# Branch B of a hybrid decoder layer: who joins the transposed halves of P, and at which slots

## The chip, the cores and the metric

The kernel runs on one core of a Trainium2 chip. A core has five engines that run their own instruction queues in order and wait for each other through semaphores: TensorE (PE in the profile, with its weight loads as PEld), VectorE (DVE), ScalarE (ACT), GpSimd (POOL) and SyncE (SP), which here issues most of the transfers. The metric is the device time of one execution in microseconds (us), lower is better.

## The reference

One decoder layer over 512 tokens of width 2048, all in float32. One projection of the normalised input feeds three token mixers side by side, and their outputs are gated, projected, weighted and summed:

```python
proj = hn @ w_in                      # 512 x 2048 by 2048 x 12300
ya = sliding_window_attention(...)    # A: 12 query heads, 4 key heads, window 128
yb = forgetting_attention(...)        # B: 12 heads of 64, causal over all 512 tokens
yc = memory_attention(...)            # C: 4 heads of 128 over 256 memory tokens
y = g0 * (ya*silu(za) @ w_a) + g1 * (yb*silu(zb) @ w_b) + g2 * (yc*silu(zc) @ w_c)
return x + y @ w_out
```

The change touches branch B alone. For each of its 12 heads

```python
sc = q @ k.T * scale + c_q[:, None] - c_k[None, :]   # c: running sum of log forget gates
p = softmax(where(key <= query, sc, NEG))            # 512 x 512, causal
out = p @ v                                          # 512 x 64
```

## The kernel before, in words

**The stream and its clock.** TensorE works through one long stream of projection products (line 301): a unit is 24 matmuls, a value is split into a high and a low part, and a product takes three matmuls (high by high, high by low, low by high). A chunk of eight units makes one 512 x 384 or 512 x 512 block of the projection, in four PSUM banks that ScalarE (and for V also VectorE) evicts at its end. The next chunk writes the same banks. While the stream runs, attention work is slipped in by a clock that counts the stream's own matmuls: every three of them are a tick of half a slot, so a slot is six matmuls of the stream. What is due by the clock is written at that place into every engine's queue, so a slot number fixes the order of instructions in each queue, and no time. The order is manual: no scheduler changes it.

**The stages.** The 12 heads of B run in two halves of six. The first half runs while the chunks qB1, kB1 and vB1 are computed (24 units, 96 slots), the second half while qA0, qA1 and kvA are computed (again 96 slots). `BASES_B` gives each head its base slot within such a stage, `STEPS_B` the offset of each of its steps from that base.

**A head of B, step by step.** Offsets are those of the kernel before, in slots from the head's base.
- GpSimd builds the four blocks of bias `biB` (lines 621 and 622, offsets -2 to 1.5). They have two buffers, so the third waits until VectorE has used the first.
- At 0, 1, 3.5 and 5, for four blocks of 128 queries: TensorE makes the scores `sB` (lines 585 and 586), VectorE adds the bias and finds the row minimum into `pB` (line 609), ScalarE exponentiates (line 612, one slot later), VectorE divides by the row sum (lines 589 and 590, three slots later).
- `halves`: GpSimd copies the 32-bit values of `pB` as 16-bit numbers into `s1B` (lines 632 and 634), all the low halves of the words first and then all the high ones, so that each can be transposed as 16-bit data.
- `send`, 10.5: SyncE issues one transposing transfer (line 639) from `s1B` to `s2B`.
- `join`, 16.5: a copy (line 645) puts the two transposed halves together again, into 32-bit words in `ptB`: 128 x 2560 16-bit values, read in a row and written with every second place left out.
- `s2`, 18: ScalarE casts `ptB` to the high part `phB` (line 651). `s2l`, 19: VectorE subtracts it for the low part `plB` (line 654).
- `s3`, 20.5: TensorE makes eight products with V into `avB` (line 663), by turns with `phB` and `plB`. ScalarE copies the lower half of the bank out (line 575, `avsB`, one slot later) and VectorE adds the halves (line 579, 3.5 slots after that).

**What is shared.** `phB` and `plB` have one buffer, as have `s1B`, `s2B` and `ptB`. V (the tile `V`) has one buffer too, which the first half's heads read and which the eviction of vB1 at the stage's end writes anew. In the same queues stand, for each unit, ScalarE's cast of the next weights (line 212) and VectorE's low part of them (line 215), and for each query and key chunk the evictions (line 446), squares (line 411), sums (lines 415, 416), GpSimd's power (line 382) and VectorE's scaling (line 422).

Of the kernel before, what the change touches and what calls it, by code (L numbers as in the profile page):

```python
# [31 lines left out]
UK = 2  # L32
BOFF = (0, 512, 1024, 896)

BASES_B = ((14, 26, 38, 46, 58, 70), (14, 26, 38, 46, 58, 70))
BASES_A = (12.5, 17, 23.5, 37.5, 43, 48.5, 52, 70.5, 75.0, 79.5, 81, 89)
BASES_C = (12.0, 19.5, 28.0, 33.5)
STEPS_B = (-12, -8.5, -2, -1.5, 0, 1, 1.0, 1.5, 3.5, 5, 10.5, 16.5, 18, 19, 20.5, 4.5)
STEPS_A = (-5.0, -1.0, -0.5, -1.5, 6.5, 8, 11, -6.5)
STEPS_C = (-8, -3.5, 0.5, 1, 8.0, 4.5, 10)  # L40

# [16 lines left out]
def tile_hybrid_block(ctx, tc, xT, x, memT, mem, ng, mng, w_in, b_forget, gqa, gka, sinks, gqb, gkb, gqc, gkc,  # L58
                      w_mem, w_a, w_b, w_c, w_out, relm, out):
    nc = tc.nc  # L60
    ve, ac, po, pe, sy = nc.vector, nc.scalar, nc.gpsimd, nc.tensor, nc.sync
# [7 lines left out]
    def f32(ap):  # L69
        return ap.bitcast(F32)  # L70
# [15 lines left out]
    def ysv(br, i):  # L86

        if (br, i // 2) not in ys:
            ys[br, i // 2] = place({"B": 0, "A": 3, "C": 6}[br] + i // 2, f"ys{br}{i // 2}")
        return ys[br, i // 2][:, i % 2, :]  # L90
# [52 lines left out]
    def later(dt, f):  # L143
        at_slot(clock[0] + dt, f)
# [16 lines left out]
    def release(*names):  # L161
        for n in names:
            free[n] += 1
# [227 lines left out]
    def u16(ap):  # L391
        return ap.bitcast(U16)

    def spare(n, name, dtype=F32, cols=1280):

        return tokp.tile([P, 1280 * 4 // mybir.dt.size(dtype)], dtype, tag=f"X{n}", bufs=1, name=name)[:, :cols]
# [134 lines left out]
    def sbank(name):  # L531
        return bank(1, name)

    def avbank(name):
        return bank(0, name)
# [35 lines left out]
    def pv_out(av, dst, half, name, slots):  # L571

        def copy():
            tmp = tokp.tile([P, 512], F32, tag="sc", bufs=2, name=name)
            ac.copy(tmp[0:64, :], av[64:128, :])
            later(slots[1], lambda: add(tmp))

        def add(tmp):
            ve.tensor_tensor(dst, av[0:64, :], tmp[0:64, :], op=ALU.add)
            release("T")  # L580
        later(slots[0], copy)

    def scores(dst, q, kh, kl, i, ks):
        qs = slice(i * P, (i + 1) * P)
        pe.matmul(dst, q[:, qs], kh[:, ks], start=True, stop=False)
        pe.matmul(dst, q[:, qs], kl[:, ks], start=False, stop=True)

    def scaled(p, den, i, engine=po):
        ve.reciprocal(den[:, 4 + i:5 + i], den[:, i:i + 1])  # L589
        engine.tensor_scalar(p, p, den[:, 4 + i:5 + i], None, op0=ALU.mult)  # L590

    def head_B(h, kv):

        s = {}

        def s1(i):
            q, kh, kl, v, hv, cb = kv()
            if i == 0:
                s["p"] = at.p.tile([P, 1280], F32, tag="P", bufs=2, name=f"pB{h}")
                s["den"] = cp.tile([P, 16], F32, tag="den", bufs=2, name=f"denB{h}")  # L600
            p, den = s["p"], s["den"]
            o = (0, 128, 384, 768)[i]
            n = (i + 1) * P
            bi = s["b", i]
            sb = sbank(f"sB{h}_{i}")
            scores(sb[:, :n], q, kh, kl, i, slice(0, n))
            pi = p[:, o:o + n]
            nm = den[:, 8 + i:9 + i]
            ve.tensor_tensor_reduce(out=pi, in0=sb[:, :n], in1=bi[:, :n], scale=-1.0, scalar=3.0e38,  # L609
                                    op0=ALU.add, op1=ALU.min, accum_out=nm)  # L610
            release("bias")
            later(EXP_B, lambda: ac.activation(pi, pi, AF.Exp, bias=nm, scale=-1.0, accum_out=den[:, i:i + 1]))  # L612
            later(DIV_B, lambda: scaled(pi, den, i, ve))
            s["p", i] = pi
            if i > 1:
                later(DIV_B + 0.5, lambda: halves(i))

        def sb(i):
            n = (i + 1) * P
            bi = at.p.tile([P, S], F32, tag="bias", bufs=2, name=f"biB{h}_{i}")  # L620
            po.tensor_scalar(bi[:, :n], kv()[5][:, :n], -1.0, cq[:, i, h:h + 1], op0=ALU.mult, op1=ALU.add)
            po.affine_select(out=bi[:, i * P:n], in_=bi[:, i * P:n], pattern=[[-1, P]], compare_op=ALU.is_ge,
                             fill=NEG, base=0, channel_multiplier=1)
            s["b", i] = bi

        def halves(i):

            if i == 0:
                s["s1"] = spare(0, f"s1B{h}", U16, 2560).rearrange("p (e j n) -> p e j n", e=2, n=P)
            src = u16(s["p", i]).rearrange("p (j n e) -> p e j n", n=P, e=2)  # L630
            n = min(i + 1, 3)
            po.tensor_copy(s["s1"][:, :, i:i + 3 * n - 2:3, :], src[:, :, :n, :])
            if i == 3:
                po.tensor_copy(s["s1"][:, :, 7:8, :], src[:, :, 3:4, :])
                release("P")

        def send():
            s["s2"] = spare(1, f"s2B{h}", U16, 2560)
            sy.dma_start_transpose(out=s["s2"].rearrange("p (x n) -> p x n", n=P),
                                   in_=s["s1"].rearrange("p e j n -> p (e j n)"))  # L640
            release("S1")

        def join():
            s["t"] = spare(2, f"ptB{h}")
            ac.copy(u16(s["t"]).rearrange("p (n e) -> p e n", e=2), s["s2"].rearrange("p (e n) -> p e n", e=2))  # L645
            release("S2")

        def s2():
            s["hi"] = at.p.tile([P, 1280], F32R, tag="PH", bufs=1, name=f"phB{h}")
            s["lo"] = at.p.tile([P, 1280], F32R, tag="PL", bufs=1, name=f"plB{h}")  # L650
            ac.copy(s["hi"], s["t"])

        def s2l():
            ve.tensor_tensor(s["lo"], s["t"], f32(s["hi"]), op=ALU.subtract)
            release("RW")

        def s3():
            q, kh, kl, v, hv, cb = kv()
            av = avbank(f"avB{h}")
            for j in range(NT):  # L660
                n = S - j * P
                for w, t in enumerate((s["hi"], s["lo"])):
                    pe.matmul(av[:, j * P:], v[:, j, hv, :], t[:, BOFF[j]:BOFF[j] + n],  # L663
                              start=(j == 0 and w == 0), stop=(j == NT - 1 and w == 1))
            pv_out(av, ysv("B", h // 2)[(h % 2) * 64:(h % 2) * 64 + 64, :], h % 2, f"avsB{h}", PV_B)

        def done():
            release("Q", "KH", "KL", *(["cb"] if h % 2 else []))

        o = STEPS_B  # L670
        steps = [(o[2], ["bias"], lambda: sb(0)), (o[3], ["bias"], lambda: sb(1)), (o[4], ["P"], lambda: s1(0)),
                 (o[5], [], lambda: s1(1)), (o[6], ["bias"], lambda: sb(2)), (o[7], ["bias"], lambda: sb(3)),
                 (o[8], [], lambda: s1(2)), (o[15], ["S1"], lambda: (halves(0), later(0.5, lambda: halves(1)))), (o[9], [], lambda: (s1(3), done())),
                 (o[10], ["S2"], send), (o[11], ["RW"], join), (o[12], ["PT"], s2), (o[13], [], s2l),
                 (o[14], ["T"], lambda: (s3(), release("PT")))]
        return steps
# [119 lines left out]
    def plan(bases, heads):  # L796

        t0 = clock[0]
        for base, steps in zip(bases, heads, strict=True):
            Chain(t0 + base, steps)  # L800

    def heads_B(part):
        cache = {}

        def prep(pr, which):
            if which == "q":
                cb = at.p.tile([P, 2, S], F32, tag="cb", bufs=2, name=f"cb{part}{pr}")
                for e in range(2):
                    h = part * 6 + 2 * pr + e
                    sy.dma_start(out=cb[:, e, :], in_=cdram[h:h + 1, :].partition_broadcast(P))  # L810
                cache[pr, "c"] = cb
            src = toks[f"{which}B{part}"]
            tb = heads_T(src, pr * P, NT, f"t{which}B{part}{pr}")
            f, g = (q_stack, "qb") if which == "q" else (k_stack, "kb")
            cache[pr, which] = [f(tb, e, gains[g], f"{which}B{part}{pr}{e}") for e in range(2)]
            later(LOW_Q if which == "q" else LOW_K, lambda: release("T"))

        def mk(hl):
            def kv():
                q, k = cache[hl // 2, "q"][hl % 2], cache[hl // 2, "k"][hl % 2]  # L820
                return q, k[0], k[1], toks[f"vB{part}"], hl, cache[hl // 2, "c"][:, hl % 2, :]
            base = BASES_B[part][hl]
            pre = [(PREP_Q[part][hl // 2] - base, ["T", "Q", "Q", "cb"], lambda: prep(hl // 2, "q")),
# [752 lines left out]
    for e in range(2):  # L1576
        kt = at.p.tile([P, S], F32R, name=f"kl{e}", tag=f"kl{e}")
        po.memset(f32(kt[64:128, :]), 0.0)
        klt.append(kt)
    plan(BASES_B[0], heads_B(0))  # L1580
    run(n_p1, n_p2)
    plan(BASES_B[1], heads_B(1))
    run(n_p2, n_p3)
# [56 lines left out]
```

## Time and profile before

| | |
|---|---|
| time, median of 3 runs | 1539.13 us (1537.29 to 1539.95) |
| the profiled execution: its time | 1539.29 us |
| the profiled execution: its span | 1537.5 us |
| PE busy in the span | 1485.7 us (97%) |
| DVE, ACT, POOL busy | 1094.1, 761.6, 217.2 us |
| mean granted TensorE clock | 0.983 of full speed |

The span is the time from the first to the last instruction, so 1.8 us of the execution lie around it. The profile counts a matmul that is pipelined behind another as busy for its whole length, so a busy PE is not a PE at its peak. Times in the trace count from the start of the span. The two halves of branch B lie between 109.3 and 426.2 us: the chunk qB1 begins at 109.32, qA0 at 265.60, and the next chunk after kvA at 426.22.

### The profile page before, as it was taken

How to read it: one execution, taken by the hardware profiler on the slowest of the kernel's cores; microseconds unless marked ns; L12 is line 12 of the kernel's file. 1: busy time of each engine (PE TensorE's matmuls, PEld its weight loads, DVE VectorE, ACT ScalarE, POOL GpSimd, SP SyncE). 2: the span in 40 equal slices, each digit the busy share in tenths (PEclk: the TensorE clock that was granted, in tenths of full speed). 3: DMA queues.
4: the chain of work that ended last, by engine and by line, in shares of the span. 5: the costliest groups of instructions: out<-in, count | busy, mean ns of one | idle time of the engine just before them, and what ended most of it. 6: DMA issues, size and time to landing. Idle time of an engine off the chain costs nothing.

```text
span 1537.5 us, 20169 instructions
## 1 busy us (share of the span) xinstructions
PE 1485.7 (97%) x7073; PEld 1276.1 (83%) x7073; DVE 1094.1 (71%) x1862; ACT 761.6 (50%) x1200; POOL 217.2 (14%) x283
## 2 busy tenths in 40 slices
PE   9999778978999999999999999999999999999998
PEld 9998778977778888888888888888888888888887
DVE  5485555565567876657978787878787655679997
ACT  5546465556555766445544444444444444336442
POOL 0122441243223433000000000000000021110000
PEclk9999799988999999999999999999999999999999
DMA  8774334534434522358667676767676867775784
GB/s 281 222 223 113 100 86 131 151 86 114 137 107 139 163 83 86 93 192 262 224 188 251 195 250 194 252 191 251 193 247 191 292 180 236 250 239 192 253 284 154
DMA packets 166733, 287.35 MB, mean 187 GB/s; under 512 B 53596, under 2 KB 93148, under 8 KB 166632
## 3 DMA queue, kind: packets, MB, share of 16 engines
q1 hardware_dynamic: 161592, 269.54, 56.3%
q10 hardware_dynamic: 5040, 16.53, 3.2%
q8 instruction: 55, 0.90, 0.3%
q14 instruction: 46, 0.38, 0.1%
HBM read 244.58 MB, written 31.48 MB: 180 GB/s over the span
## 4 chain that ended last, share of the span: by engine, by line
PE 88%; ACT 6%; DVE 3%; issue 2%; POOL 1%; DMA 0%; SPq 0%; DVEq 0%; POOLq 0%; ACTq 0%
PE P L1113 40%; PE z L301 11%; PE uB L1113 4%; PE uA L1113 4%; PE qB L301 4%; PE vB L301 3%; PE kB L301 3%; PE qC L301 3%; PE uC L1113 3%; PE qA L301 3%; PE mem L301 3%; PE kvA L301 2%; ACT ptB L645 2%; PE avB L663 1%; DVE wc L215 1%
## 5 line engine op out<-in xcount | busy, mean ns | idle before, releaser
L215 DVE TENSOR_TENSOR wc<-wa,wb 128x512 fp32r<-128x512 f32 (+2 forms) x252 | 148.7, 629 | 110.4 <-ACT wb L212 105.3
L212 ACT CAST wb<-wa 128x512 fp32r<-128x512 f32 (+2 forms) x252 | 130.4, 566 | 132.2 <-PE z L301 34.5
L1155 ACT CAST wa<-rawl 128x1024 fp32r<-128x1024 f32 x85 | 89.5, 1053 | 207.5 <-DVE rawl L1045 158.4
L1045 DVE TENSOR_TENSOR rawl<-rawl 128x512 f32<-128x512 f32 x256 | 177.0, 692 | 5.7 <-DMA rawl<-in_w_out_dram 1.3
L1158 DVE TENSOR_TENSOR wc<-rawl,wa 128x1024 fp32r<-128x1024 f32 x85 | 105.0, 1235 | 52.0 <-ACT wa L1155 50.3
L1429 POOL TENSOR_TENSOR y<-y,gA 128x512 f32<-128x512 f32 x16 | 28.1, 1786 | 727.6 <-DVE gA L1427 727.6
L1158 DVE TENSOR_TENSOR we<-rawl,wd 128x512 fp32r<-128x512 f32 (+1 forms) x128 | 122.1, 954 | 4.1 <-ACT wd L1155 0.5
L1155 ACT CAST wd<-rawl 128x512 fp32r<-128x512 f32 (+1 forms) x128 | 106.8, 835 | 22.7 <-DVE rawl L1045 17.2
L301 PE MATMUL z<-ah,wb 128*128 128x512 f32 x256 | 101.9, 398 | 1.5 <-DVE V_vA L462 1.5
L301 PE MATMUL z<-ah,wc 128*128 128x512 f32 x256 | 99.9, 390 | 0.0
L301 PE MATMUL z<-al,wb 128*128 128x512 f32 x256 | 99.9, 390 | 0.0
L1155 ACT CAST wb<-rawl 128x1024 fp32r<-128x1024 f32 x43 | 45.3, 1054 | 87.8 <-DVE rawl L1045 70.5
L1113 PE MATMUL P<-wd,xhx 128*128 128x512 f32 x192 | 74.7, 389 | 0.0
L1113 PE MATMUL P<-wd,xlx 128*128 128x512 f32 x192 | 74.7, 389 | 0.0
L1113 PE MATMUL P<-we,xhx 128*128 128x512 f32 x192 | 74.7, 389 | 0.0
L1158 DVE TENSOR_TENSOR wb<-rawl,wb 128x1024 fp32r<-128x1024 f32 x43 | 52.5, 1222 | 25.6 <-ACT wb L1155 25.3
L1042 DVE TENSOR_TENSOR R<-P,R 128x512 f32<-128x512 f32 (+1 forms) x90 | 57.0, 673 | 6.9 <-PE P L1113 6.2
L301 PEld LDWEIGHTS z<-ah,wb 128*128 128x128 f32 x256 | 48.1, 188 | 11.2 <-DVE V_vA L462 1.9
L301 PEld LDWEIGHTS z<-ah,wc 128*128 128x128 f32 x256 | 48.1, 188 | 10.3
L590 POOL TENSOR_SCALAR pA<-pA,denA 128x256 f32<-128x256 f32 (+1 forms) x48 | 44.6, 946 | 78.8 <-DVE denA L589 78.8
L301 PEld LDWEIGHTS z<-al,wb 128*128 128x128 f32 x256 | 48.2, 188 | 9.0
L612 ACT ACTIVATE pB<-pB,denB 128x128 f32<-128x128 f32 (+3 forms) x48 | 27.0, 562 | 56.7 <-DVE denB L609 56.6
(411 smaller groups left out, 4287.9 us busy)
## 6 DMA issues: line engine op xcount, KB each, us to landing
rawl<-in_w_in_dram SPq DMA_DIRECT2D x144, 512.0 KB, 4.3
rawl<-in_w_out_dram SPq DMA_DIRECT2D x48, 512.0 KB, 4.9
wa<-in_w_in_dram SPq DMA_DIRECT2D x62, 384.0 KB, 3.6
wa<-in_w_in_dram SPq DMA_DIRECT2D x64, 256.0 KB, 3.0
rawl<-in_w_in_dram SPq DMA_DIRECT2D x48, 256.0 KB, 4.1
gates<-R ACTq DMA_DIRECT2D x24, 512.0 KB, 7.7
wa<-in_w_in_dram SPq DMA_DIRECT2D x16, 512.0 KB, 3.7
wa<-in_w_mem_dram SPq DMA_DIRECT2D x16, 512.0 KB, 3.6
```

The costliest lines, as they stand in the source:

```text
L212: ac.copy(hi[:, :n], raw[:, i, :n])
L215: ve.tensor_sub(lo[:, :n], raw[:, i, :n], f32(hi[:, :n]))
L301: pe.matmul(pb, a, m, start=b in fresh, stop=last and not todo[b])
L590: engine.tensor_scalar(p, p, den[:, 4 + i:5 + i], None, op0=ALU.mult)
L612: later(EXP_B, lambda: ac.activation(pi, pi, AF.Exp, bias=nm, scale=-1.0, accum_out=den[:, i:i + 1]))
L645: ac.copy(u16(s["t"]).rearrange("p (n e) -> p e n", e=2), s["s2"].rearrange("p (e n) -> p e n", e=2))
L1042: ve.tensor_tensor(out, a, b, op=ALU.add)
L1045: ve.tensor_tensor(out, a, b, op=ALU.subtract)
L1113: pe.matmul(*args, **kw)
L1155: ac.copy(hi[:, :k, :], src)
L1158: return lambda: ve.tensor_tensor(lo[:, :k, :], src, f32(hi[:, :k, :]), op=ALU.subtract)
L1429: po.tensor_tensor(y, y, g, op=ALU.add)
```

## The change

Two things are changed. `join` runs on GpSimd instead of ScalarE. And the slots: `join` is one slot earlier after its head's base (15.5 for 16.5), the cast `s2` one later (19 for 18), the subtraction `s2l` 1.5 later (20.5 for 19), and the products with V `s3` 4.5 later (25 for 20.5). The fifth head of each half begins one slot earlier (57 for 58) and the sixth two (68 for 70). Every step before `join` keeps its offset from its head's base.

```diff
-BASES_B = ((14, 26, 38, 46, 58, 70), (14, 26, 38, 46, 58, 70))
+BASES_B = ((14, 26, 38, 46, 57, 68), (14, 26, 38, 46, 57, 68))
-STEPS_B = (-12, -8.5, -2, -1.5, 0, 1, 1.0, 1.5, 3.5, 5, 10.5, 16.5, 18, 19, 20.5, 4.5)
+STEPS_B = (-12, -8.5, -2, -1.5, 0, 1, 1.0, 1.5, 3.5, 5, 10.5, 15.5, 19, 20.5, 25, 4.5)
@@ def join():
             s["t"] = spare(2, f"ptB{h}")
-            ac.copy(u16(s["t"]).rearrange("p (n e) -> p e n", e=2), s["s2"].rearrange("p (e n) -> p e n", e=2))
+            po.tensor_copy(u16(s["t"]).rearrange("p (n e) -> p e n", e=2), s["s2"].rearrange("p (e n) -> p e n", e=2))
             release("S2")
```

What this does to the queues is shown at three places. The numbers behind names are buffer numbers.

ScalarE in the first stage, where chunk qB1 ends and kB1 begins. `t_qB` are the evictions of its banks (`qB_2` and `qB_3` the third and fourth), the four rows of `kB` the keys of the third and fourth head, `pB` an exponential of the second head, `ptB` and `phB` the first head's join and cast. Before:

```order
L645 COPY ptB_1628<-s2B_1539 128x2x1280
L446 ACTIVATE t_qB_1603<-qB_2_1240,rstds 128x384
L558 ACTIVATE kB_1650<-tkB_1645,g_kb 64x512
L561 ACTIVATE kB_1650<-tkB_1645,g_kb 64x512
L558 ACTIVATE kB_1653<-tkB_1645,g_kb 64x512
L561 ACTIVATE kB_1653<-tkB_1645,g_kb 64x512
L446 ACTIVATE t_qB_1603<-qB_3_1241,rstds 128x384
L411 ACTIVATE sq_qB_1661<-t_qB_1603 128x384
L612 ACTIVATE pB_1557,denB_1558<-pB_1557,denB_1558 128x512
L651 CAST phB_1664<-ptB_1628 128x1280
L212 CAST wb_1667<-wa_1595 128x384 x2
```

The same place now:

```order
L446 ACTIVATE t_qB_1603<-qB_2_1240,rstds 128x384
L558 ACTIVATE kB_1650<-tkB_1645,g_kb 64x512
L561 ACTIVATE kB_1650<-tkB_1645,g_kb 64x512
L558 ACTIVATE kB_1653<-tkB_1645,g_kb 64x512
L561 ACTIVATE kB_1653<-tkB_1645,g_kb 64x512
L446 ACTIVATE t_qB_1603<-qB_3_1241,rstds 128x384
L411 ACTIVATE sq_qB_1661<-t_qB_1603 128x384
L612 ACTIVATE pB_1557,denB_1558<-pB_1557,denB_1558 128x512
L212 CAST wb_1664<-wa_1595 128x384 x2
L651 CAST phB_1690<-ptB_1613 128x1280
```

The join no longer stands ahead of the evictions, and the cast stands behind the next weights' cast.

GpSimd at the same time, now: `biB` are the last two biases of the second head, `ptB` the join of the first, `s1B` the second head's halves, `nr_qB` a power for the chunk's normalisation.

```order
L621 TENSOR_SCALAR biB_2_1574<-cb_1245,cq 128x384
L622 AFFINE_SELECT biB_2_1574<-biB_2_1574 128x128
L621 TENSOR_SCALAR biB_3_1582<-cb_1245,cq 128x512
L622 AFFINE_SELECT biB_3_1582<-biB_3_1582 128x128
L645 COPY ptB_1613<-s2B_1539 128x2x1280
L632 COPY s1B_1630<-pB_1557 128x2x128
L632 COPY s1B_1630<-pB_1557 128x2x2x128
L632 COPY s1B_1630<-pB_1557 128x2x3x128
L382 TENSOR_TENSOR nr_qB_1605<-nr_qB_1605,mhalf 128x6
```

Before, the row of `ptB` was not in this queue, and the rest stood in the same order. So the join now stands ahead of all the halves of the next head.

TensorE at the end of the first stage, now: the first bank of vB1 is complete, and the products with V of the sixth head come next, still with the old V.

```order
L301 MATMUL vB_0_2228<-wb_2556,ah_80 128x384
L301 MATMUL vB_0_2228<-wc_2557,ah_80 128x384
L301 MATMUL vB_0_2228<-wb_2556,al_88 128x384
L663 MATMUL avB_2606<-phB_2545,V_vB_1191 128x512
L663 MATMUL avB_2606<-plB_2546,V_vB_1191 128x512
L663 MATMUL avB_2606<-phB_2545,V_vB_1191 128x384
```

Before, the sixth head's products stood 2.5 slots (15 matmuls of the stream) earlier, ahead of the end of that bank. In both kernels every head's products stand exactly at base plus offset: none was pushed to a later slot by a tile or bank that was still taken.

## The prediction

> **What bounds the kernel now.** I read the page's slices first, to see where PE isn't full, then the stages, then who PE waits for.
>
> ```profile
> PE   9999778978999999999999999999999999999998
> PEclk9999799988999999999999999999999999999999
> ```
>
> One slice is 38.4 us. PE is full everywhere but in slices 5 to 10, and the granted clock drops in slices 5, 9 and 10: that is branch B. The stages (columns: length, then busy time and instructions of PE, PEld, DVE, ACT, POOL, then clock, DMA share, GB/s):
>
> ```profile
> 0.00:109.30 109.30, 107.14 (x597) 105.12 (x598) 65.82 (x158) 55.56 (x108) 16.68 (x25) 1.00 0.76 239
> 109.30:265.60 156.30, 132.73 (x699) 126.45 (x697) 84.20 (x205) 86.82 (x152) 52.63 (x86) 0.91 0.42 114
> 265.60:426.20 160.60, 140.82 (x697) 126.43 (x697) 94.69 (x222) 89.64 (x156) 50.45 (x83) 0.93 0.43 119
> 500.00:600.00 100.00, 99.49 (x536) 84.14 (x535) 72.06 (x201) 68.84 (x166) 42.13 (x46) 1.00 0.36 109
> ```
>
> The two B stages last 156.3 + 160.6 = 316.9 us and PE is busy for 273.6 of them, so 43.3 us are idle. No other engine is above 60% there, and transfers move half of what they do in the first stage. So PE is held up by order and latency. The last row, with branch A's heads, shows that PE can be full with DVE at 72%. Who PE waits for in 109.3 to 426.2 (total us, times, longest):
>
> ```profile
> PE avB L663 <- DVE plB L654: 24.5, 11, 2.7
> PE avB L663 <- ACT phB L651: 10.0, 8, 2.7
> PE qA L301 <- ACT t_qA L446: 3.1, 2, 2.5
> PE kB L301 <- ACT t_qB L446: 3.1, 2, 2.5
> PE vB L301 <- ACT t_kB L446: 1.5, 1, 1.5
> PE kvA L301 <- ACT t_qA L446: 0.8, 1, 0.8
> ```
>
> These six rows are 43.0 us, all of the idle time. 34.5 us are waits of the products with V for their two operands. The other 8.5 are waits for evictions at the ends of chunks.
>
> The idle time has a second price. PE from 178 to 188 us:
>
> ```profile
> 178.62 0.49 PE L663 MATMUL avB<-phB,V_vB 128*128 128x512 f32 x1 [2.67 <-ACT phB L651]
> 181.50 0.79 PE L663 MATMUL avB<-plB,V_vB 128*128 128x512 f32 x1 [2.38 <-DVE plB L654]
> 185.93 0.52 PE L301 MATMUL kB<-wb,ah 128*128 128x384 f32 x1
> 186.25 0.52 PE L301 MATMUL kB<-wc,ah 128*128 128x384 f32 x1
> 187.68 0.33 PE L301 MATMUL kB<-wb,ah 128*128 128x384 f32 x1
> 187.85 0.33 PE L301 MATMUL kB<-wc,ah 128*128 128x384 f32 x1
> ```
>
> After two waits matmuls start 0.32 us apart, and 0.17 apart from 187.5 on. The trace has nine such stretches, all between 153 and 382 us. Asked for as windows, the first and the sum:
>
> ```profile
> 153.30:163.50 10.20, 7.23 (x23) 6.38 (x22) 6.27 (x14) 4.33 (x9) 6.77 (x9) 0.50 0.45 104
> sum 51.20, PE 41.97 PEld 38.98 DVE 24.27 ACT 14.93 POOL 26.48; mean PE 4.66 PEld 4.33 DVE 2.70 ACT 1.66 POOL 2.94
> ```
>
> For 51.2 us the clock is at half, and PE works in 42.0 of them, so they cost 21.0 us.
>
> **The change part by part.** First, why the products wait. The three steps before them take, for one head:
>
> ```profile
> L645 ACT COPY ptB<-s2B 128x2560 uint16<-128x2560 uint16 x12 | 37.3, 3107 | 0.0
> L651 ACT CAST phB<-ptB 128x1280 fp32r<-128x1280 f32 x12 | 15.1, 1254 | 0.1
> L654 DVE TENSOR_TENSOR plB<-ptB,phB 128x1280 fp32r<-128x1280 f32 x12 | 17.8, 1485 | 0.0
> L215 DVE TENSOR_TENSOR wc<-wa,wb 128x384 fp32r<-128x384 f32 x79 | 41.7, 568 | 37.3 <-ACT wb L212 37.1
> ```
>
> The first three make 3.1 + 1.25 + 1.49 = 5.85 us in a row, without any queueing; a pair of weight subtractions (the fourth row, 1.1 us) can stand ahead of the low part. From join to products the old slots leave 20.5 - 16.5 = 4 slots. A slot is six stream matmuls of 0.17 us, so 1.03 us; with the heads' own matmuls it is on average (316.9 - 43.3 - 21.0)/192 = 1.32 us, from the two stages' 192 slots. 4 slots are 4.1 to 5.3 us: too few by 0.6 to 1.7 us even with empty queues, and the measured 34.5/12 = 2.9 us a head adds the queues.
>
> **Later products.** Now there are 25 - 15.5 = 9.5 slots, 9.8 us of the stream alone and 12.5 with the average of the heads' matmuls. They have to hold the join on GpSimd, 1.25, 1.1 and 1.49 us.
>
> **The join on GpSimd** is in no row. The nearest are GpSimd's own 16-bit copies, which read with a stride and write in a row, and what ScalarE pays for writing with a stride:
>
> ```profile
> 135.28 0.83 POOL L632 COPY s1B<-pB 128x768 uint16<-128x768 uint16 x1 [1.56 <-DVE pB L590]
> 136.05 0.40 POOL L634 COPY s1B<-pB 128x256 uint16<-128x256 uint16 x1
> L1503 ACT COPY y4s<-yh 128x512 uint16<-128x512 uint16 x8 | 6.2, 773 | 12.5 <-DMA yh<-gC 12.3
> L1155 ACT CAST wa<-rawl 128x1024 fp32r<-128x1024 f32 x85 | 89.5, 1053 | 207.5 <-DVE rawl L1045 158.4 <-PE P L1113 37.9 <-PE uA L1113 5.6
> L1429 POOL TENSOR_TENSOR y<-y,gA 128x512 f32<-128x512 f32 x16 | 28.1, 1786 | 727.6 <-DVE gA L1427 727.6
> ```
>
> From 256 to 768 values GpSimd takes 0.43/512 = 0.84 ns a value and 0.19 us at the start: 2560 values make 2.3 us, the lower bound. ScalarE's joins go from 773 ns for 512 to 3107 for 2560, 1.14 ns a value, its plain casts from 1053 ns for 1024 to 1254 for 1280, 0.79 ns: strided 16-bit writes cost it 1.45 times. With that factor GpSimd's join is 0.19 + 2560 x 0.84 x 1.45 = 3.3 us. The upper bound is GpSimd's dearest streaming row, the add of two operands, 1786/512 = 3.5 ns a value: 8.9 us. I take 3.3 us, since type and kind of copy are the same. Then 3.3 + 1.25 + 1.1 + 1.49 = 7.1 us of the 9.8: **all 34.5 us of waits go**, with 2.7 us to spare, and the cast isn't held up either (it stands 3.5 slots, 3.6 us, behind the join).
>
> **Is the join's data there a slot earlier?** The first head's last scores, and the transfer's median from issue to landing:
>
> ```profile
> 130.83 0.39 PE L585 MATMUL sB<-kB,qB 128*128 128x512 f32 x1
> s2B<-s1B SPq DMA_TRANSPOSE x12, 4.1
> ```
>
> That head's halves end at 136.05 + 0.40 = 136.45 us, so the data lands at 140.6, 9.8 us after the scores; the join stands 15.5 - 5 = 10.5 slots behind them, 10.8 us and more. It fits by 1 us or more.
>
> **What stands behind the join on GpSimd.** It is the next head's halves, then biases, then powers.
>
> ```profile
> POOL s1B L632 <- DVE pB L590: 82.5, 29, 9.5
> ```
>
> GpSimd waits 82.5 us for DVE before halves, so it has the room: 103.1 us busy of 316.9, plus 12 x 3.3 = 40 makes 143 of some 258. In the worst place (third head's join between the fourth head's halves) a 3.3 us join moves the fourth head's transfer by that much, and that head's join still stands 5 slots behind its transfer. Cost nothing. If that cover is gone, the late transfer holds the join, and a rival below prices it. DVE and ACT: DVE's 178.9 us stay, 69% of the shorter stage; ACT loses 37.3 of 176.5.
>
> **The evictions at chunk ends** waited behind the join on ACT:
>
> ```profile
> 145.31 3.10 ACT L645 COPY ptB<-s2B 128x2560 uint16<-128x2560 uint16 x1
> 148.29 0.56 ACT L446 ACTIVATE t_qB<-qB,rstds 128x384 f32<-128x384 f32 x1
> 148.76 0.67 ACT L558 ACTIVATE kB<-tkB,g_kb 64x512 fp32r<-64x512 f32 x1
> 151.53 0.58 ACT L446 ACTIVATE t_qB<-qB,rstds 128x384 f32<-128x384 f32 x1
> 147.05 0.34 PE L301 MATMUL kB<-wb,ah 128*128 128x384 f32 x1
> 152.17 0.44 PE L301 MATMUL kB<-wb,ah 128*128 128x384 f32 x1 [2.47 <-ACT t_qB L446]
> ```
>
> Without the join the third bank is evicted at once, and the four key rows still take 151.53 - 148.76 = 2.8 us ahead of the fourth bank. Their transposes stand three stream matmuls ahead of the chunk's end at 147.05, so they can start near 146.5, and the fourth eviction ends near 149.9. PE wants that bank nine matmuls into the new chunk, at 148.6: 1.3 us stay of 3.1. The same holds for qA (3.1), which has the keys at the same slot. The waits for t_kB and in kvA (1.5 and 0.8) have a join just ahead and no keys, and go. So 8.5 - 2.6 = **5.9 us saved**.
>
> **The sixth head** now has its products at slot 68 + 25 = 93 of 96, behind the first bank of the chunk with V, and the eviction that writes V anew has to wait until they have read it. Eight products and no more, from the second stage:
>
> ```profile
> 399.84 0.50 PE L663 MATMUL avB<-plB,V_vB 128*128 128x512 f32 x1 [2.09 <-DVE plB L654]
> 400.95 0.45 PE L301 MATMUL kvA<-wb,ah 128*128 128x512 f32 x1
> ```
>
> That is 1.1 us a stage, **2.2 us lost** if nothing hides it; the bound below is 0, since three slots remain until the bank is wanted. Moving the fifth and sixth heads up costs nothing that I see.
>
> **The clock.** Each of the nine half-speed stretches begins within 2 us of a wait of avB. The lone wait of 2.09 us at 399.84 has none behind it (the last ends at 382), so the 1.3 us left at two chunk ends shouldn't have one either. **21.0 us saved.**
>
> The sum, against the profiled execution: 1539.3 - 34.5 - 5.9 - 21.0 + 2.2 = 1480.1 us. That execution is 0.2 us above the median of the runs, so I predict 1480 us for the median.
>
> **The rivals.**
> 1. *The join is dear on GpSimd*, 8.9 us. Then the low part is ready 8.9 + 1.25 + 1.1 + 1.49 = 12.7 us behind the join where PE needs it after 9.8 to 12.5, midway 11.2: 1.5 us a head, 18 us, and of the clock 21 x 18/34.5 = 11 us. 1480 + 29 = 1509. For it: no row shows a strided 16-bit write on GpSimd. Against it: its strided reads run at 0.84 ns.
> 2. *The half clock stays.* The waits go, but what is left of them (1.3 us twice, V at the stages' ends, small ones) still trips it, or its cause is another: 1480 + 21 = 1501. For it: no wait of avB is longer than 2.7 us, and 2.09 us alone did nothing. Against it: the clock is 1.00 in the stages without such waits. The Trainium skill (TensorE: Matmul & The Clock Gate, Part 1) says the clock falls to half after a whole idle window of about 3.4 us and returns after a busy one. By that rule waits of at most 2.7 us would not be the cause, and this rival would hold; the trace, where clock and waits go together, doesn't bear it out so far.
> 3. *Slower: GpSimd's queue becomes the chain.* Join, halves, transfer and landing of one head follow on those of the last if the join holds the queue until its data lands. A head now has 316.9/12 = 26.4 us; GpSimd's own work is 103.1/12 = 8.6, the landing 4.1, so it decides from a join of 26.4 - 12.7 = 13.7 us (5.4 ns a value). At 15 us it is 12 x 1.3 = 16 us slower, 1555. For it: an add of two operands takes 3.5 ns already, and the join's write is of a kind no row has. Against it: 5.4 ns is beyond any row shown.
> 4. *No gain*: the products still wait as long because the cast, held by a late join, holds weights and exponentials on ACT: 1539. Against it: 3.5 slots for the join.
>
> **How the numbers follow.** The forecast has 0.80 (its own range 1469 to 1491: 11 us lower if the rest of the chunk-end waits and the slower first matmul after each wait go as well, 11 higher with a wait of 1 us for most heads), the dear join 0.08, the half clock 0.06, GpSimd's queue 0.04, no gain 0.02. The range 1469 to 1509 takes in the first three and both bounds of the join. A measurement here tells about 0.2% from no change. Faster by more: 0.80 + 0.08 + 0.06 = 0.94; within it 0.02; slower 0.04.
>
> **What would show it.** In the profile after: avB's two waits below 5 us in all; a clock of 1.00 in both B stages, which last some 129 us each; no ACT row at line 645, a POOL row of 2.3 to 4 us there; the wait for t_qB halved. Wrong would be a join above 9 us, waits of line 301 for weights (wb, wc), or waits of sB for biases behind the join.

## The result, and the profile after

| | before | after |
|---|---|---|
| time, median | 1538.27 us (1537.29 to 1539.95) | 1498.88 us (1498.74 to 1499.70) |
| ratio to before | 1 | 0.9744, 95% interval 0.9727 to 0.9761 |
| the profiled execution: its span | 1537.5 us | 1497.9 us |
| mean granted TensorE clock | 0.983 | 0.994 |

The change makes the kernel 39.4 us faster. The forecast was 1480 us: its sign holds, but 18.9 us of the gain didn't come. (The median of the kernel before is over four runs here, over three further up.)

The first two rows of the page's slices, of the kernel after, one slice now 37.4 us:

```profile
PE   9999989989999999999999999999999999999998
PEclk9999999999999999999999999999999999999999
```

No slice is below 8 tenths any more, and no slice's mean clock below 9. The two halves of branch B as windows, of the kernel after (columns as in the prediction):

```profile
108.92:243.40 134.48, 125.02 (x697) 120.95 (x697) 101.34 (x205) 69.15 (x146) 82.58 (x92) 0.96 0.50 132
243.40:387.12 143.72, 134.26 (x697) 121.66 (x697) 111.49 (x222) 72.07 (x150) 78.93 (x89) 0.98 0.48 134
sum 278.20, PE 259.28 PEld 242.61 DVE 212.84 ACT 141.22 POOL 161.51; mean PE 129.64 PEld 121.30 DVE 106.42 ACT 70.61 POOL 80.76
```

The halves fell from 316.9 to 278.2 us, where some 258 had been forecast. Outside them the span is 1497.9 - 278.2 = 1219.7 us, before 1537.5 - 316.9 = 1220.6: whatever went or came lies in branch B. Two columns were not expected. The clock isn't 1.00. And DVE, none of whose instructions was moved to it, is busy for 212.84 us instead of 178.9.

Who PE waits for there, in the kernel after (total us, times, longest):

```profile
PE kB L301 <- DVE wc L215: 4.0, 2, 2.1
PE kB L301 <- ACT t_qB L446: 2.5, 1, 2.5
PE qA L301 <- ACT t_qA L446: 2.5, 1, 2.5
PE kvA L301 <- DVE wc L215: 2.4, 1, 2.4
PE qA L301 <- DVE wc L215: 1.9, 2, 1.0
PE vB L301 <- DVE wc L215: 1.8, 1, 1.8
PE qA L301 <- ACT wb L212: 1.6, 2, 1.0
PE vB L301 <- ACT t_kB L446: 0.9, 1, 0.9
PE kvA L301 <- ACT t_qA L446: 0.6, 1, 0.6
PE sB L585 <- DVE denB L609: 0.5, 1, 0.5
...
```

No product with V waits any more. In its place the stream itself waits: 10.1 us for the low part of its weights (wc), 1.8 for the high part (wb, with 0.2 in a row not shown), and 6.5 us for evictions, of which 2.6 had been forecast.

Why wc is late shows in the groups by shape, GpSimd's join and DVE's subtraction in branch B:

```profile
L645 POOL COPY ptB<-s2B 128x2560 uint16<-128x2560 uint16 x12 | 38.3, 3188 | 8.7 <-DVE x3s L1042 4.4 <-DMA s2B<-s1B 4.3
L215 DVE TENSOR_TENSOR wc<-wa,wb 128x384 fp32r<-128x384 f32 x78 | 57.0, 771 | 7.9 <-ACT wb L212 7.6
```

The join takes 3188 ns, close to the 3.3 us forecast. But the subtraction went from a mean of 568 to 771 ns. One join in the timeline of the kernel after (start, length, engine, line, operation):

```profile
168.31 3.10 POOL L645 COPY ptB<-s2B 128x2560 uint16<-128x2560 uint16 x1
...
169.60 0.14 DVE L589 RECIPROCAL denB<-denB 128x1 f32<-128x1 f32 x1
169.78 1.84 DVE L590 TENSOR_SCALAR pB<-pB,denB 128x384 f32<-128x384 f32 x1
171.66 1.51 DVE L548 SCALAR_TENSOR_TENSOR qB<-tqB,gs_qb,qB 64x512 fp32r<-64x512 f32 x2
173.20 1.23 DVE L215 TENSOR_TENSOR wc<-wa,wb 128x384 fp32r<-128x384 f32 x2
...
173.82 0.45 PE L301 MATMUL kB<-wc,ah 128*128 128x384 f32 x1 [2.11 <-DVE wc L215]
```

The division of line 590, a 128 x 384 block that took 0.43 us on average before, starts 1.5 us into the join and ends at 171.62, 0.2 us after the join's end at 171.41. Query rows and two subtractions stand behind it on DVE, and PE, which needs the first of them, waits 2.11 us.

The other joins show the same, and mostly with the subtraction itself. Under each of the twelve joins one DVE instruction lasts until 0.2 to 0.5 us after the join's end: seven subtractions of line 215, two scalings of line 422, this one division, and two more rows (lines 1045 and 1060). All but the division take two operands from SBUF. Five of the 128 x 384 subtractions last 2.3 to 3.4 us under a join, where 0.57 us is usual. Rows that take an operand from PSUM aren't longer under a join: line 609 at 168.38 takes 0.69 us, its usual time. It looks as if the join held DVE. The experiments test that.

### The profile page after: what moved, and what is told of

The parts are those of the page before. It is cut to its first block, busy times and chain, and to the rows that moved or that the text cites. A ratio compares the mean times of both kernels' runs of the same rounds, so it can differ in the third digit from the quotient of the medians.

```text
span 1497.9 us, 20162 instructions
## 1 busy us (share of the span) xinstructions
PE 1471.0 (98%) x7073; PEld 1266.5 (85%) x7073; DVE 1127.7 (75%) x1862; ACT 726.0 (48%) x1188; POOL 276.5 (18%) x295
## 4 chain that ended last, share of the span: by engine, by line
PE 84%; DVE 5%; POOL 4%; issue 3%; ACT 2%; DMA 1%; POOLq 0%; DVEq 0%; ACTq 0%
PE P L1113 41%; PE z L301 11%; PE uB L1113 4%; PE uA L1113 4%; PE vB L301 4%; PE qB L301 4%; PE qC L301 3%; PE uC L1113 3%; PE kB L301 2%; PE mem L301 1%; PE qA L301 1%; DVE wc L215 1%; PE kvA L301 1%; POOL s1B L632 1%; POOL biB L621 1%
## 5 line engine op out<-in xcount | busy, mean ns | idle before, releaser
L215 DVE TENSOR_TENSOR wc<-wa,wb 128x512 fp32r<-128x512 f32 (+2 forms) x252 | 167.9, 704 | 66.9 <-ACT wb L212 63.0
L1155 ACT CAST wd<-rawl 128x512 fp32r<-128x512 f32 (+1 forms) x128 | 106.8, 834 | 23.8 <-DVE rawl L1045 21.2
```

Source lines behind the costliest of these rows:

```text
L215: ve.tensor_sub(lo[:, :n], raw[:, i, :n], f32(hi[:, :n]))
L1155: ac.copy(hi[:, :k, :], src)
```

## The experiments

The theory, **blocking**: while GpSimd's copy runs, it keeps DVE's divisions and subtractions from their data, and what they make comes late to PE. Its rival, **queue**: DVE is only late because biases and halves wait behind the join in GpSimd's queue. A second rival, called crowding in the expectations: the stages are shorter, and DVE's queue is simply full, whoever joins. Another question is what of the gain belongs to the slots and what to the engine.

**The new slots with the join back on ScalarE** (`act_new_slots`), the change without its engine:

```diff
-            po.tensor_copy(u16(s["t"]).rearrange("p (n e) -> p e n", e=2), s["s2"].rearrange("p (e n) -> p e n", e=2))
+            ac.copy(u16(s["t"]).rearrange("p (n e) -> p e n", e=2), s["s2"].rearrange("p (e n) -> p e n", e=2))
```

> The changed kernel with its new slots, but the join back on ScalarE (one word undone). Theory 'blocking': the 10.1 us in which TensorE waits for low parts of weights (wc, line 215) come from VectorE being held while GpSimd's 3.2 us join runs. Then they go here (below 3 us), line 215 goes back from 0.77 to about 0.57 us for 128x384, and the products with V still don't wait, since 9.5 slots hold 3.1 + 1.25 + 1.1 + 1.5 us; the waits for evictions at chunk ends go up from 6.0 to 6 to 8.5 us, as the join stands ahead of them again: 1485 to 1492 us. Rival 'crowding': the stage is shorter and VectorE's queue is simply full, whoever joins. Then the waits for wc stay at 8 us or more, and with the dearer evictions it is 1500 to 1506 us.

It takes 1485.96 us (1485.40 to 1486.37), a ratio of 0.9658 (0.9644 to 0.9673): the fastest kernel of the study, 12.9 us faster than the change. The halves of B as windows, and DVE's subtraction over the whole run, of this kernel:

```profile
108.32:236.97 128.65, 121.84 (x697) 116.50 (x697) 87.07 (x205) 85.59 (x152) 60.48 (x86) 1.00 0.52 139
236.97:372.33 135.36, 131.63 (x697) 120.83 (x697) 97.27 (x222) 89.12 (x156) 58.58 (x83) 0.99 0.51 142
```

```profile
L215 DVE TENSOR_TENSOR wc<-wa,wb 128x384 fp32r<-128x384 f32 x108 | 59.0, 587 | 17.6 <-ACT wb L212 17.2
```

The same 205 + 222 instructions of DVE take 184.3 us here and 212.8 in the change; the subtraction has 587 ns, and 710 over the whole run of the change. PE waits 1.8 us for wc instead of 10.1, in stages that are shorter still, so crowding falls. No 128 x 384 subtraction takes longer than 0.96 us. The waits for evictions are 5.6 us, where 6 to 8.5 had been expected. So the gain is the slots' (1538 to 1486), and moving the join to GpSimd costs 13 us of it.

**The old slots with the join on GpSimd** (`pool_old_slots`), the engine alone, changed in the kernel before:

```diff
-            ac.copy(u16(s["t"]).rearrange("p (n e) -> p e n", e=2), s["s2"].rearrange("p (e n) -> p e n", e=2))
+            po.tensor_copy(u16(s["t"]).rearrange("p (n e) -> p e n", e=2), s["s2"].rearrange("p (e n) -> p e n", e=2))
```

> The kernel before with its old slots, but the join on GpSimd. The old 4 slots (4.1 to 5.3 us) have to hold 3.2 + 1.25 + 1.5 us. If the slots carry the gain, the products with V still wait 25 to 35 us and the clock still halves: 1525 to 1540 us. If the engine carries it: waits below 15 us and 1510 us or less.

1540.79 us, 1.0013 (1.0004 to 1.0023): no gain at all. PE's waits for the products' operands in this kernel:

```profile
PE avB L663 <- DVE plB L654: 24.6, 11, 2.8
PE avB L663 <- ACT phB L651: 11.9, 6, 3.6
```

These are 36.5 us, before 34.5; both they and the time lie just above what was expected of the slots as the cause. Where the products come too early, another engine for the join doesn't help them.

**The join in four pieces on GpSimd** (`join_in_4`): the same values, and more time on GpSimd, but no single copy is long.

```diff
-            po.tensor_copy(u16(s["t"]).rearrange("p (n e) -> p e n", e=2), s["s2"].rearrange("p (e n) -> p e n", e=2))
+            dst = u16(s["t"]).rearrange("p (n e) -> p e n", e=2)
+            src = s["s2"].rearrange("p (e n) -> p e n", e=2)
+            for c in range(0, 1280, 320):
+                po.tensor_copy(dst[:, :, c:c + 320], src[:, :, c:c + 320])
```

> The changed kernel with GpSimd's join cut into four copies of 128x640 values, same work. Theory 'blocking', held for one instruction: VectorE waits for at most one piece (0.7 to 0.9 us) instead of up to 3.1, its longest division (line 590) falls from 1.8 to about 1.2 us, the waits for wc from 10 to 3 to 6 us: 1488 to 1495 us. If GpSimd keeps VectorE out over all four pieces: 1497 to 1501 us. Rival 'crowding': no change or up to 4 us slower from three more starts of 0.2 us, 1498 to 1503 us.

1491.57 us, 0.9694 (0.9679 to 0.9708): 7.3 us faster than the change. Its pieces, and the divisions (ns minimum/median/maximum) in this kernel:

```profile
L648 POOL COPY ptB<-s2B 128x640 uint16<-128x640 uint16 x48 | 47.3, 1051 | 8.7 <-DVE x3s L1045 4.4 <-DMA s2B<-s1B 4.4
```

```profile
L590 DVE TENSOR_SCALAR pB<-pB,denB x48: 285/420/1100, 126.5 to 347.7; 128x128 f32<-128x128 f32 x12, 128x256 f32<-128x256 f32 x12, 128x384 f32<-128x384 f32 x12, 128x512 f32<-128x512 f32 x12
```

GpSimd is busy with the join for 47.3 us instead of 38.3, so all that stands behind it in the queue comes later, and yet the kernel is faster. A longest division of 1.10 us (1.84 in the change) and a longest 128 x 384 subtraction of 1.21 us (3.42 in the change) go with pieces of 1.05 us on average. That speaks for blocking and against the queue as the main cost: 7.3 of the 12.9 us go away with the long single copies. The waits for wc fell less than expected, from 10.1 to 8.0 us; evictions fell to 2.8.

**The join twice** (`join_twice`), the second time over the same places:

```diff
             po.tensor_copy(u16(s["t"]).rearrange("p (n e) -> p e n", e=2), s["s2"].rearrange("p (e n) -> p e n", e=2))
+            po.tensor_copy(u16(s["t"]).rearrange("p (n e) -> p e n", e=2), s["s2"].rearrange("p (e n) -> p e n", e=2))
```

> The changed kernel with the join made twice on GpSimd (the second writes the same values again). Theory 'blocking': VectorE can be held twice as often, and the next head's halves come 3.2 us later; waits for wc go up from 10 to 18 us or more, and line 215 gets dearer again: 1508 to 1530 us. Rival 'crowding': GpSimd has the room (about 50% busy in the stage) and the cast has 2.7 us to spare, so at most the products with V wait 0.5 us a head: 1498 to 1506 us.

1522.69 us, 0.9898 (0.9883 to 0.9912), 23.8 us slower than the change; the waits for wc are 16.4 us, those for evictions 11.7. The longest division takes 3.05 us, one whole copy of 3.1 and not two: DVE comes in between two copies. This run can't part the two theories by itself, since the queue is longer too.

**A useless copy, and a useless fill, beside ScalarE's join** (`act_extra_copy`, `act_extra_fill`). Both start from the fastest kernel; at slot 13 GpSimd writes 2048 values into places that the join overwrites. The copy reads them from SBUF (the diff shows it), the fill has `po.memset(d, 0)` in its place and reads nothing. In `join`, ScalarE copies as in `act_new_slots`, and the line with `spare` has moved to `extra`.

```diff
+        def extra():
+            s["t"] = spare(2, f"ptB{h}")
+            d = u16(s["t"]).rearrange("p (n e) -> p e n", e=2)[:, :, :1024]
+            po.tensor_copy(d, u16(ah[0].rearrange("p k n -> p (k n)")).rearrange("p (e n) -> p e n", e=2))
...
-                  (o[10], ["S2"], send), (o[11], ["RW"], join), (o[12], ["PT"], s2), (o[13], [], s2l),
+                  (o[10], ["S2"], send), (13, ["RW"], extra), (o[11], [], join), (o[12], ["PT"], s2), (o[13], [], s2l),
```

The copy:

> The join on ScalarE at the new slots, and at slot 13 of each head an extra GpSimd copy of 128x2048 16-bit values from an old input tile into ptB (written with a stride, overwritten by the join): nobody needs it, it only occupies GpSimd for some 2.5 us and reads and writes SBUF. Theory 'blocking': VectorE's two-operand and SBUF-to-SBUF rows are held again (line 590 up to 1.5 us or more, line 215 near 0.7 us), and the time goes from 1486 back to 1492 to 1500 us. Rival: what mattered in the changed kernel was the chain through GpSimd's join to the cast; then a copy nobody waits for costs at most the 1 to 2 us of later biases: 1486 to 1489 us.

The fill:

> The same with a fill (memset) of the same 128x2048 places in the extra copy's stead, which writes and reads nothing. If GpSimd holds VectorE by reading SBUF alone: 1486 to 1488 us, lines 215 and 590 as without it. If it does so by any access, or just by being busy ahead of the biases: as the extra copy, in proportion to its length.

The copy makes 1499.77 us (0.9747, 0.9731 to 0.9763), the fill 1498.18 (0.9733, 0.9718 to 0.9748): both give back about what the change's join does, 13.8 and 12.2 us, although nobody reads what they write. GpSimd's copy, DVE's subtraction and the divisions with the copy:

```profile
L646 POOL COPY ptB<-ah 128x2048 uint16<-128x2048 uint16 x12 | 30.8, 2570 | 5.1 <-DVE plB L658 5.1
L215 DVE TENSOR_TENSOR wc<-wa,wb 128x384 fp32r<-128x384 f32 x108 | 70.6, 693 | 15.2 <-ACT wb L212 14.8
...
L590 DVE TENSOR_SCALAR pB<-pB,denB x48: 285/420/2768, 126.5 to 359.2; 128x128 f32<-128x128 f32 x12, 128x256 f32<-128x256 f32 x12, 128x384 f32<-128x384 f32 x12, 128x512 f32<-128x512 f32 x12
```

And the same three with the fill:

```profile
L646 POOL MEMSET ptB<- 128x2048 uint16 x12 | 29.4, 2446 | 5.1 <-DVE plB L658 5.1
L215 DVE TENSOR_TENSOR wc<-wa,wb 128x384 fp32r<-128x384 f32 x108 | 59.0, 596 | 18.1 <-ACT wb L212 17.7
...
L590 DVE TENSOR_SCALAR pB<-pB,denB x48: 285/421/2771, 126.1 to 355.9; 128x128 f32<-128x128 f32 x12, 128x256 f32<-128x256 f32 x12, 128x384 f32<-128x384 f32 x12, 128x512 f32<-128x512 f32 x12
```

Under either the longest division lasts 2.77 us, against 0.58 without them. The subtraction, which reads two operands from SBUF, is held by the copy (693 ns) and not by the fill (596, against 587 without); two subtractions that run wholly inside the fill at 271.26 us take 1.03 us together. So DVE is held, and it depends on what both instructions read. The Trainium skill (SBUF — State Buffer, Who interferes with whom) says just that: VectorE's second pair of ports is GpSimd's as well and locked for a whole instruction, a VectorE instruction with two SBUF inputs clashes with a GpSimd instruction that reads, and one in a two-port mode, which `tensor_scalar` (here the division) can enter, with any. These rows agree with it.

The two times don't give the price of the hold, though. Somebody does wait for the useless instruction: it writes the buffer that ScalarE's join writes next, so that the join, and ScalarE's queue behind it, waits until it is done. From ScalarE's waits with the fill:

```profile
ACT ptB L649 <- POOL ptB L646: 8.3, 6, 2.2
```

With the copy it is 8.5 us. DVE is busy in the halves for 206.2 us with the copy and for 191.0 with the fill, against 184.3 without either. So the fill keeps DVE some 7 us longer, the copy some 22, and both cost nearly the same. How the 12 and 14 us divide between the held DVE, the waiting ScalarE and what stands later in GpSimd's queue isn't measured.

**Keys later** (`act_keys_later`, `keys_later`). The two waits of 2.5 us for evictions stay in both kernels, behind four key rows on ScalarE. Here the keys go 1.5 slots later, with ScalarE's join and with GpSimd's.

```diff
-PREP_K = ((6.5, 31.5, 51.5), (7, 31.5, 51.5))
+PREP_K = ((6.5, 33, 51.5), (7, 33, 51.5))
```

> The join on ScalarE at the new slots (the faster kernel of the runs so far, 1486 us), and the preparation of the third and fourth heads' keys at slot 33 instead of 31.5 in both stages, so that its four ScalarE rows (2.8 us) stand behind the eviction of the chunk's fourth bank. Theory: the two waits of 2.5 us for t_qB and t_qA at a chunk's end are these four rows. They fall below 0.7 us each, and the time to 1480 to 1483 us. Rival: the rows only move the wait to the keys' own users or to the weights; 1485 to 1488 us.

> The changed kernel (join on GpSimd) with the same move of the keys. Theory: the same 5 us go, and the waits for low parts of weights (10 us) stay, as they come from VectorE being held by GpSimd: 1492 to 1496 us. Rival: the evictions are late because VectorE's held queue delays the exponential ahead of them, so that the waits stay near 2 us: 1497 to 1500 us.

1488.20 us (0.967, 0.9655 to 0.9684) with ScalarE's join, 2.2 us more than without, which is not clear of noise, since the intervals overlap; 1502.50 us (0.9761, 0.9747 to 0.9776) with GpSimd's, 3.6 more than the change, at the edge of it. No gain came in either. In both the two waits for t_qB and t_qA are gone, and what is late next takes their place; from PE's waits with ScalarE's join:

```profile
PE sB L586 <- DVE kl L559: 2.5, 2, 1.4
```

The next head's scores wait for the keys' low part, and products and weights for DVE behind that. With GpSimd's join the waits for wc stayed at 10.1 us, so they don't hang on the evictions. Both theories had the time fall by some 5 us with these waits, and it didn't. The first time lies at the upper end of its rival's range, the second above it.

**Only the products later** (`act_only_products`): the new bases, and of the steps `s3` alone at 25; join, cast and subtraction stand at 16.5, 18 and 19 as before, the join on ScalarE. Against `act_new_slots`:

```diff
-STEPS_B = (..., 15.5, 19, 20.5, 25, 4.5)
+STEPS_B = (..., 16.5, 18, 19, 25, 4.5)
```

> The kernel before with the new bases and one new offset alone: the products with V at 25 instead of 20.5; join on ScalarE at 16.5, cast at 18, subtraction at 19 as before. Theory: the gain is the room between join and products (8.5 slots, 8.8 us and more for 5.9 to 7 us of work), so the waits of the products stay gone: 1484 to 1490 us, as with all the new slots (1486). Rival: the cast and the subtraction, a slot and a half later than the join, keep ScalarE and VectorE from waiting in their queues; at the old offsets VectorE is held for the cast and weights come late: 1493 to 1503 us.

1503.82 us, 0.9773 (0.9757 to 0.9789). No product waits, but PE waits 6.5 us for wb. ScalarE's timeline in this kernel, and PE's instruction that waits:

```profile
171.00 3.11 ACT L645 COPY ptB<-s2B 128x2560 uint16<-128x2560 uint16 x1
174.14 1.38 ACT L547 ACTIVATE qB<-tqB,gs_qb 64x512 fp32r<-64x512 f32 x2
175.54 0.72 ACT L612 ACTIVATE pB<-pB,denB 128x512 f32<-128x512 f32 x1
...
176.26 1.24 ACT L651 CAST phB<-ptB 128x1280 fp32r<-128x1280 f32 x1
177.41 0.92 ACT L212 CAST wb<-wa 128x384 fp32r<-128x384 f32 x2
...
177.97 0.44 PE L301 MATMUL kB<-wb,ah 128*128 128x384 f32 x1 [3.45 <-ACT wb L212]
```

Join, query rows, an exponential and the head's cast stand in one row ahead of the weights' cast, 6.4 us without a gap. With the join a slot earlier, the cast a slot and the subtraction 1.5 slots later (`act_new_slots`) that row is broken up. The three offsets together are worth 1503.8 - 1486.0 = 18 us; of PE's waits, those for wb are 6.5 us here and 2.9 there, those for the softmax's row minimum (denB) 4.1 and none.

**The old bases** (`act_old_bases`), the fifth and sixth head at 58 and 70 again, ScalarE's join. Against `act_new_slots`:

```diff
-BASES_B = ((14, 26, 38, 46, 57, 68), (14, 26, 38, 46, 57, 68))
+BASES_B = ((14, 26, 38, 46, 58, 70), (14, 26, 38, 46, 58, 70))
```

> All new offsets with the join on ScalarE, but the fifth and sixth heads at their old bases (58 and 70): the sixth head's products come at slot 95 of 96, and the eviction that overwrites V waits for them. Theory: each stage's end then waits 1 to 3 us for V: 1488 to 1493 us against 1486. Rival: the bases are without effect, 1484 to 1488 us.

1487.46 us, 0.9668 (0.9654 to 0.9683): 1.5 us more than with the new bases, and the intervals overlap. They hardly matter.

**ScalarE's join in two pieces** (`act_join_in_2`), at 15.5 and 17, to let ScalarE's other work in between:

```diff
-                  (o[11], ["RW"], join),
+                  (o[11], ["RW"], join), (17, [], lambda: join(640)),
```

> The join on ScalarE at the new slots, cut into two copies of 128x1280 values at 15.5 and 17, so that evictions at chunk ends can come between. Theory: the evictions wait for at most half a join; the waits for t_qB, t_qA and t_kB (5.6 us) fall by 1 to 3 us: 1482 to 1485 us. Rival: those waits are the four key rows and late exponentials, so only the start of a second copy is added: 1485 to 1488 us.

1487.23 us, 0.9667 (0.9653 to 0.9682), 1.3 us more than in one piece, again with overlapping intervals. The evictions wait 6.2 us, with the whole join 5.6. At the first chunk's end the third bank is evicted earlier (at 144.76 us, with the whole join at 146.36), but the second piece then stands ahead of the four key rows, and the fourth bank comes at 149.51 instead of 149.60. So two pieces don't help; how much of these waits is the join's, this run can't tell.

## Why the prediction was right or wrong

- **Waits of the products with V, 34.5 us: right.** Of the two rows none is left. Slots do it, with either engine.
- **The join's price, 3.3 us: right,** at 3188 ns on average. The bound of 8.9 us and with it the rival of the dear join fall, as does GpSimd's queue as a chain, which needed 13.7 us. GpSimd's busy time as a whole was mis-sized: 161.5 us, where the step counted 143. With ScalarE's join at the new slots it is 119.1, before 103.1, so most of the excess isn't the join's.
- **"What stands behind the join on GpSimd ... Cost nothing" and "DVE's 178.9 us stay": wrong, and the main failure.** The step looked at GpSimd's own queue and counted room there. It didn't ask what a 3 us copy does to its neighbour, whose instructions it holds until it ends: DVE's busy time rose to 212.8 us (184.3 with ScalarE's join), 12.4 us of new waits of PE arose (wc 10.1, wb 1.8, denB 0.5), and the engine's move costs 12.9 us of the 18.9 that were missing. The prediction's own list of what would show it wrong had the place, "waits of line 301 for weights".
- **Evictions, 5.9 us saved: 2.0.** They went from 8.5 to 6.5 us. The step had the third bank evicted at once when the join is gone from ScalarE. The kernel after:

```profile
142.00 3.87 DVE L215 TENSOR_TENSOR wc<-wa,wb 128x384 fp32r<-128x384 f32 x2 [0.69 <-ACT wb L212]
142.09 3.41 POOL L645 COPY ptB<-s2B 128x2560 uint16<-128x2560 uint16 x1
145.79 0.54 DVE L609 CUSTOM_DVE_ANT_0 pB<-sB,biB 128x384 f32<-128x384 f32 x1
...
146.38 0.62 ACT L612 ACTIVATE pB<-pB,denB 128x384 f32<-128x384 f32 x1 [1.96 <-DVE denB L609]
...
146.99 0.56 ACT L446 ACTIVATE t_qB<-qB,rstds 128x384 f32<-128x384 f32 x1
147.45 0.67 ACT L558 ACTIVATE kB<-tkB,g_kb 64x512 fp32r<-64x512 f32 x1
...
150.24 0.58 ACT L446 ACTIVATE t_qB<-qB,rstds 128x384 f32<-128x384 f32 x1
```

  ScalarE stands idle for 1.96 us, waiting for a block of the softmax ahead of the third bank's eviction; the four key rows then still take 150.24 - 147.45 = 2.8 us. The block is late because its row minimum (line 609) stands on DVE behind two subtractions, and the second of these is held until the join on GpSimd ends. With ScalarE's join the pair takes 1.23 us at this place. So the join left ScalarE's queue, and its time came back there as a wait for DVE. Where the chunk qA0 ends, the same rows stand again (a pair of 3.87 us at 276.51, an idle time of 1.96 us before 280.89). That the two waits are 2.5 us with ScalarE's join as well has another reason: there the join itself (142.32 to 145.42) stands ahead of the same exponential.
- **Half clock, 21.0 us saved: 12.7.** Five stretches at half speed are left, 17.0 us with PE busy for 16.6, so 8.3 us are still lost. The step took from "the lone wait of 2.09 us" that smaller waits don't trip the clock. The section on the hardware shows what that wait really told. The trace of the kernel before had a sign against the step: two of its nine stretches, from 153.3 and 310.3 us, follow the two waits of 2.5 us for evictions, which end at 152.17 and 308.83, and the waits of avB beside them lie at the start of the stretch or behind it. So waits at chunk ends did set off half clock.
- **The sixth head, 2.2 us charged: 0,** its lower bound. The one wait for V, in the chunk behind the second half, is 1.0 us, and was 1.5 before. The two slots by which that head was moved up do little, as `act_old_bases` shows.
- **The sum.** In the halves PE's idle time fell from 43.3 to 278.2 - 259.3 = 18.9 us and the loss to half clock from 21.0 to 8.3: 24.4 + 12.7 = 37.1 of the 38.7 us measured there. Against the forecast of some 258 us for the halves, 12.4 are new waits, 3.9 evictions, 8.3 half clock, less the 2.2 charged for V: 22.4, where 20.5 are missing. The 2 us between weren't traced.

Of the rivals the one of the half clock was nearest in number (1501), but its story was not what happened: most of the half-speed time went, and four of the five stretches that are left follow waits for wc. The forecast's own range, 1469 to 1491, doesn't hold. That 1499 lies within 1469 to 1509 is owed to the width that the rivals gave to the range, so it is luck: what made most of the difference, the held DVE, stood in none of them. With ScalarE's join one stretch is left (clock 0.999), and the time is 6 us above the forecast.

## What to carry to other kernels

Slack for a chain of dependent steps is worth more than a faster engine for one of them: compute the chain's length from its rows, and give the consumer that many slots. Before work is moved to GpSimd, look at what VectorE does at the same time: a long GpSimd copy or fill can hold VectorE for as long as it lasts, even where GpSimd has room, so keep such copies short or put them on ScalarE if that has room. And where engines run in order, taking an instruction out of a queue only helps if what stands next in it doesn't wait, through another engine, for the same instruction.

## What the runs showed of the hardware

**The half clock goes by fixed windows.** All stretches at half speed begin on a grid of 3.41 us: in the kernel after at 150.5, 174.4, 218.8, 307.5 and 362.1 us, which are 7, 13, 26 and 16 steps of 3.413 apart, and such a grid fits the nine stretches of before, and those of the seven experiments that have more than one, to 0.05 us. What decides is how much of one such window PE is idle. Four windows of the kernel after (length, then PE's busy time; clock third from the end):

```profile
147.10:150.51 3.41, 1.30 (x8) 0.92 (x6) 1.07 (x5) 3.35 (x6) 1.21 (x2) 1.00 0.34 108
150.51:153.92 3.41, 3.05 (x10) 3.05 (x11) 3.29 (x8) 3.41 (x8) 1.28 (x1) 0.51 0.00 0
283.63:287.04 3.41, 1.66 (x9) 1.67 (x10) 2.08 (x4) 3.37 (x8) 0.00 (x0) 1.00 0.00 0
287.04:290.45 3.41, 3.41 (x23) 3.41 (x22) 3.14 (x6) 2.64 (x5) 2.30 (x2) 1.00 0.46 115
```

3.41 - 1.30 = 2.11 us idle in a window are followed by half clock, 3.41 - 1.66 = 1.75 are not. Over branch B in the eleven kernels that have such stretches, every full-speed window with more than 1.75 us idle was followed by half clock and none with less than 1.61; between them both occur. That is about half the window. So a wait's length alone says little, since the grid may cut it. The wait of 2.09 us on which the prediction's step rested, in the kernel before:

```profile
395.63:399.04 3.41, 2.12 (x10) 1.42 (x8) 1.95 (x3) 1.95 (x3) 0.00 (x0) 1.00 0.00 0
399.04:402.45 3.41, 2.61 (x14) 2.30 (x15) 2.66 (x5) 0.58 (x1) 1.56 (x2) 1.00 0.55 161
```

It lies 1.29 us in one window and 0.80 in the next, and passed for that reason. The wait of 2.45 us before 150.24 in `act_new_slots` passed in the same way, some 1.4 us in one window and some 1.0 in the next. In the kernel after, two waits of 0.99 and 0.97 us in one window were enough. The Trainium skill (TensorE: Matmul & The Clock Gate, Part 1) has the free-running window of 3413 ns, which the grid bears out, and an idle window as the cause of the fall; here a window idle for about half was enough.

**A fill holds VectorE too.** A GpSimd instruction that reads nothing from SBUF kept a division of 128 x 256, which took 0.37 us on average before, until its own end at 330.56 us, and left the subtractions alone (in `act_extra_fill`):

```profile
327.94 2.77 DVE L590 TENSOR_SCALAR pB<-pB,denB 128x256 f32<-128x256 f32 x1
328.14 2.42 POOL L646 MEMSET ptB<- 128x2048 uint16 x1
```
